# Five edits around the choice of experts: lists by bf16 products, wide products while VectorE works, classes in one comparison, a hinted first jump, the light expert's sum amid a last group

## The chip, the core and the metric

The kernel runs on one core of a Trainium2 chip. A core has a matrix engine (TensorE, PE in the profile, with PEld for its weight loads), VectorE (DVE), ScalarE (ACT), GpSimd (POOL) and SyncE (SP), which here issues the loads of the weights. Each engine has its own program and they meet by semaphores. PEq, DVEq and so on are the sequencers that run an engine's loads of registers and its jumps. The metric is the time of one execution on the device in microseconds; the kernel before took 1330.01 us, the median of three runs (1320.58 to 1333.2).

## The reference

A trunk of two layers on 256 tokens of width 1024, all f32. Each layer is a token mixer (two groups of attention heads) and a channel mixer, each followed by a normalization. The channel mixer of the first layer is a dense SwiGLU; that of the second, which the change touches, sends each token to two of eight experts:

```python
logits = (xf @ router).astype(jnp.float32)
top_v, top_i = lax.top_k(logits, TOP_K)
gates = jax.nn.softmax(top_v, axis=-1)
dense_g = jnp.sum(jax.nn.one_hot(top_i, N_EXPERTS) * gates[..., None], axis=1)
y = jnp.zeros_like(xf)
for e in range(N_EXPERTS):
    y = y + dense_g[:, e:e + 1] * swiglu(xf, wg[e], wu[e], wd[e])
```

An expert's gate and up weights are 1024 x 3584 and its down weights 3584 x 1024.

## The kernel before, in words

The tokens stand in `x_sb`, 128 to a partition block, in two blocks t = 0, 1. After the second normalization of layer 1, `route.logits(t)` transposes a block by eight products with `ident` (L118) and multiplies it with the router (L126); `route.choose(t)` ranks the eight logits on VectorE (L140 to L146) and leaves masks. Between the two stands `route.ones`, 20 bf16 products of 8 columns on PE whose result nobody reads (L133). `route.places` turns the masks into each token's place in the list of its expert, and into counts, by products with triangles (L153 to L157); VectorE then makes from the count of each expert a class from 0 to 5, `kind` (L164 to L167, by comparison with the five BOUNDS 32, 64, 96, 128, 160), and from the logits the gates (L172 to L179). `route.both` makes `pair`, which says whether two experts can be run together.

The experts run in the order of ORDER. For each, a Switch on every engine reads the class from memory into a register (L192) and jumps to the arm for that number of tokens (L1446, L1480): 32 tokens (class 0) to 256 (class 5). At an arm's end `ahead` (L1428) gives each engine's sequencer a hint which arm comes next, so that its code can be fetched ahead of the jump; the first Switch has none. The second and third experts of ORDER, HEAVY and LIGHT, run interleaved (`both`) where their classes allow it.

Inside an arm, for column blocks c = 0, 1 of the hidden width: the gate products (L1090, into "mm" banks of PSUM for few tokens), Silu, the up products (L1090, "acc" banks) and a multiplication, then the hidden rows are transposed (L1123) and the down products made (L1153, or L1023 to L1025 in three passes for classes with 128 tokens at once). The weights come in halves of 1 MB into 18 places in turn. SP loads a half into a place when PE is done with the half that stood there, in one fixed sequence over all experts; `done` is called after each group of halves.

The picked tokens of an expert come into `xg`: for the first one by products of `x_sb` with a one-hot matrix `oh` (L928, `pick`), for each later one by an indirect DMA of rows from `x_rows` into `x_sb` (`gather`, on POOL, L988) and transposes (L996). The gather needs the list of the expert's tokens. `list_tokens` makes all eight lists during the first expert, at its second column block: for each expert VectorE marks the places (L978, f32 128 x 256), and PE multiplies 128 columns of the marks by one column of token numbers (L981, f32), 32 calls. The scheduler that sets the order on each engine spreads these among the gate products of that block, since the marks have two buffers in turn. An expert's result is added to `acc` by `bring`, products with a one-hot matrix (L1010) and four sums on VectorE (L1014), at the head of the next one; the light one's by `bring_light`, handed to the heavy one as `before_end` and called after its last group of down products. After it stand `scatter_few` (L1193 to L1196, for the tokens of HEAVY beyond 128) and the next pick (L996).

In the profiled run the first expert is of class 1 (64 tokens, 447.7 to 541 us), the pair of classes 4 and 0 (549 to 776), and five experts follow, the last of class 0 from 1240.

## Time and profile before

| | |
|---|---|
| median of three runs | 1330.01 us (1320.58 to 1333.2) |
| profiled execution | 1327.82 us, its span 1326.0 us |
| mean granted TensorE clock | 0.970 |
| PE busy | 1267.2 us, 96% of the span |
| DVE, ACT, POOL busy | 459.3 (35%), 360.9 (27%), 45.3 us (3%) |
| DMA | 430.60 MB, mean 325 GB/s |

Rows of the timeline give the start and duration in us, the engine, the line, the operation with output and inputs, the tile of the array and the shape, how many instructions were put together (x), and in brackets how long the engine was idle before and who ended that. An f32 product is recorded as two instructions (the record count is twice that of the calls). The rows of a stretch give the busy time of each engine, the granted clock (1.00 is full speed), the share of time in which the DMA engines were busy, and the bytes they moved. The chain of waits goes back from the last instruction to what released it.

### The profile page before, as it was taken

Reading aid. Unit: us, or ns where it says so; the run is one execution under the profiler, and the core shown is the slowest. Engines: PE = TensorE matmul, PEld = TensorE weight load, DVE = VectorE, ACT = ScalarE, POOL = GpSimd, SP = SyncE. Lnnn points to the kernel's source line nnn. Section 1 sums busy time; section 2 is a strip of 40 time slices with the busy share of each in tenths; the row PEclk is TensorE's granted clock in tenths of the full one; section 3 lists DMA queues with packets and bytes.
Section 4 is the critical chain, followed back from the end, with each engine's and each line's share of the span. In section 5 each row is a group of like instructions: output and inputs, shape, how many; then the busy total and the mean of one; then the engine's idle time right before and its main releaser. Section 6 shows DMA issues by size and latency. Waiting matters only on the chain.

```text
span 1326.0 us, 21614 instructions
## 1 busy us (share of the span) xinstructions
PE 1267.2 (96%) x8971; PEld 777.5 (59%) x8971; DVE 459.3 (35%) x742; ACT 360.9 (27%) x638; POOL 45.3 (3%) x64
## 2 busy tenths in 40 slices
PE   9999999999998799999999999999999999999974
PEld 8978999998987454545665642443542443243331
DVE  4689455567677210336544440001010001000102
ACT  4584444453573100244543410000000000000001
POOL 1010000000001000000000000000000000000000
PEclk9999999999999889999999999999999999999985
DMA  9537455553627899989999979998999999999895
GB/s 331 203 96 258 187 190 182 178 205 136 219 96 302 312 417 406 395 363 410 408 420 418 420 297 377 361 367 330 415 418 415 413 419 415 388 420 412 337 417 241
DMA packets 98026, 430.60 MB, mean 325 GB/s; under 512 B 10403, under 2 KB 16547, under 8 KB 67244
## 3 DMA queue, kind: packets, MB, share of 16 engines
q1 hardware_dynamic: 95804, 422.75, 80.9%
q0 software_dynamic: 2032, 5.63, 1.3%
q8 instruction: 81, 1.33, 0.4%
q14 instruction: 109, 0.89, 0.2%
HBM read 427.73 MB, written 2.11 MB: 324 GB/s over the span
## 4 chain that ended last, share of the span: by engine, by line
PE 82%; DMA 6%; issue 2%; DVE 2%; ACT 1%; POOL 0%; SPq 0%; DVEq 0%; ACTq 0%; POOLq 0%
PE acc L1090 15%; PE acc L1153 15%; PE mm L1090 14%; PE mm L344 4%; PE mm L343 4%; PE mm L345 4%; PE acc L1023 3%; PE acc L345 3%; PE acc L1025 3%; PE acc L344 3%; PE acc L343 3%; PE acc L1024 3%; DMA piece<-in_moe_w_down_dram 3%; PE tr L1123 2%; DMA piece<-in_moe_w_up_dram 1%
## 5 line engine op out<-in xcount | busy, mean ns | idle before, releaser
L1090 PE MATMUL acc<-piece,xg 128*64 128x512 f32 (+5 forms) x1488 | 191.9, 502 | 0.0
L1153 PE MATMUL acc<-piece,hT 128*32 128x256 f32 (+2 forms) x1504 | 175.2, 459 | 8.9 <-DMA piece<-in_moe_w_down_dram 8.9
L307 DVE TENSOR_TENSOR wl<-piece,wh 128x1024 fp32r<-128x1024 f32 (+4 forms) x124 | 135.0, 1098 | 87.9 <-ACT wh L305 85.1
L1090 PE MATMUL mm<-piece,xg 128*64 128x512 f32 (+5 forms) x896 | 143.2, 528 | 15.1 <-issue 5.5
L305 ACT ACTIVATE wh<-piece 128x1024 fp32r<-128x1024 f32 (+4 forms) x124 | 118.1, 958 | 81.6 <-PE acc L344 40.6
L1090 PEld LDWEIGHTS acc<-piece,xg 128*32 128x32 f32 (+1 forms) x1488 | 71.4, 120 | 114.6 <-issue 101.1
L1153 PEld LDWEIGHTS acc<-piece,hT 128*32 128x32 f32 (+1 forms) x1504 | 71.0, 123 | 104.2 <-issue 72.2
L343 PE MATMUL mm<-xTh,wl 128*128 128x256 f32 x448 | 126.7, 283 | 0.0
L344 PE MATMUL mm<-xTh,wh 128*128 128x256 f32 x448 | 126.5, 282 | 0.0
L345 PE MATMUL mm<-xTl,wh 128*128 128x256 f32 x448 | 126.4, 282 | 0.0
L1104 DVE TENSOR_TENSOR hd<-hd,acc 128x512 f32<-128x512 f32 (+1 forms) x24 | 14.5, 630 | 298.7 <-PE acc L1090 297.2
L838 DVE TENSOR_TENSOR wl<-piece,wh 128x1024 fp32r<-128x1024 f32 (+1 forms) x80 | 88.1, 1117 | 76.2 <-PE acc L1025 51.0
L1090 PEld LDWEIGHTS mm<-piece,xg 128*64 128x64 f32 (+1 forms) x896 | 56.9, 131 | 96.2 <-issue 84.7
L1111 ACT ACTIVATE hT<-tr 128x512 f32<-128x512 f32 (+2 forms) x30 | 15.6, 542 | 327.9 <-PE tr L1123 315.2
L837 ACT ACTIVATE wh<-piece 128x1024 fp32r<-128x1024 f32 (+1 forms) x80 | 75.8, 973 | 68.8 <-PE acc L1024 68.6
L343 PEld LDWEIGHTS mm<-xTh,wl 128*128 128x128 f32 x448 | 85.0, 190 | 0.2
L344 PEld LDWEIGHTS mm<-xTh,wh 128*128 128x128 f32 x448 | 84.2, 188 | 0.2
L345 PEld LDWEIGHTS mm<-xTl,wh 128*128 128x128 f32 x448 | 84.2, 188 | 0.0
L1169 DVE COPY hd<-acc 32x256 f32<-32x256 f32 (+2 forms) x12 | 6.6, 554 | 163.4 <-ACT hd L1169 107.5
L343 PE MATMUL acc<-wh,xTl 128*128 128x512 f32 (+2 forms) x128 | 46.7, 365 | 0.0
L345 PE MATMUL acc<-wl,xTh 128*128 128x512 f32 (+2 forms) x128 | 46.3, 363 | 0.0
L344 PE MATMUL acc<-wh,xTh 128*128 128x512 f32 (+2 forms) x128 | 46.2, 361 | 0.0
(474 smaller groups left out, 1648.2 us busy)
## 6 DMA issues: line engine op xcount, KB each, us to landing
piece<-in_moe_w_down_dram SPq DMA_DIRECT2D x95, 1024.0 KB, 15.5
piece<-in_moe_w_gate_dram SPq DMA_DIRECT2D x60, 1024.0 KB, 14.1
piece<-in_moe_w_up_dram SPq DMA_DIRECT2D x58, 1024.0 KB, 16.2
piece<-in_moe_w_up_dram SPq DMA_DIRECT2D x30, 768.0 KB, 10.2
piece<-in_moe_w_gate_dram SPq DMA_DIRECT2D x29, 768.0 KB, 8.5
piece<-in_moe_w_up_dram SPq DMA_DIRECT2D x28, 512.0 KB, 10.1
piece<-in_moe_w_gate_dram SPq DMA_DIRECT2D x26, 512.0 KB, 9.5
piece<-in_ffn_w_gate_dram SPq DMA_DIRECT2D x5, 2048.0 KB, 7.8
```

The costliest lines, as they stand in the source:

```text
L305: hi = act.activation(h, src, AF.Copy)
L307: return hi, dve.tensor_sub(lo, src, h.bitcast(F32))
L343: pe.matmul(ps, lt[1], rt[0], start=start, stop=False)
L344: pe.matmul(ps, lt[0], rt[0], start=False, stop=False)
L345: pe.matmul(ps, lt[0], rt[1], start=False, stop=stop)
L837: act.activation(h, src, AF.Copy)
L838: dve.tensor_sub(lo, src, h.bitcast(F32))
L1023: pe.matmul(ps, lt[1], rt[0], start=start, stop=False)
L1024: pe.matmul(ps, lt[0], rt[0], start=False, stop=False)
L1025: return pe.matmul(ps, lt[0], rt[1], start=False, stop=stop)
L1090: pe.matmul(self.ps[b][q * self.n:(q + 1) * self.n, c0:c0 + (jb - ja) * w], self.tokens(k), block[:, ja - j0:jb - j0, cols], **at)
L1153: latest["down"] = pe.matmul(y[g * self.n:(g + 1) * self.n, c + q:c + q + b], self.hidden(u, j), v[:, j, i * w + q:i * w + q + b], **at)
```

## The change

None of the five edits changes what is computed.

- `route.ones` makes 2 products instead of 20. A new `meanwhile` makes products of 512 columns, f32, whose result nobody reads: three behind the logits of the first block, two behind those of the second, one behind the places.
- `places` hands on the counts. `first` makes the one-hot matrix of the first expert right behind the places; `classes` makes all classes by one comparison of 128 x 40 elements with a tile `bounds` (filled by five memsets on POOL) and one reduction; the gates come after it.
- At the first Switch, the first half of the pick is made, the class of the first expert is loaded on each engine, and a hint is given on each (on PE behind the last product of that half). Then come the second half of the pick, the loads for the other experts, and `pair`.
- The token lists: `mark_tokens` makes all 16 marks in bf16 at the head of the first expert, in a tile "hT" that is free then, and `list_tokens` multiplies them in one go between the gate and the up products of the first column block, by two columns (token number and one). The two gathers for the pair move with it.
- `before_end`, the light expert's sum, is called in the last group of down products after the first part's turn, no more behind the group; and the pick that follows the pair goes to "acc" banks and is copied by ScalarE alone.

```diff
                          pattern=[[1, E], [-1, E]], channel_multiplier=0)
+        self.bounds = tmp.tile([P, len(BOUNDS)], F32, name="bounds")
+        for j, b in enumerate(BOUNDS):
+            gp.memset(self.bounds[:, j:j + 1], b + 0.5)
         self.lg = tmp.tile([P, 2, E], F32, name="lg")
...
         for k in range(KD):
-            pe.matmul(ps[:, :E], xT[:, k], self.rt[:, k], start=k == 0, stop=k == KD - 1)
+            self.latest = pe.matmul(ps[:, :E], xT[:, k], self.rt[:, k], start=k == 0, stop=k == KD - 1)
         return dve.tensor_copy(self.lg[:, t], ps[:, :E])
...
+    def meanwhile(self, tc, ps_pool, ident, x, n):
+
+        ps = ps_pool.tile([P, 512], F32, name="acc")
+        with tc.issue_after(self.latest.ins):
+            for _ in range(n):
+                self.nc.tensor.matmul(ps, ident, x, start=True, stop=True)
+
     def choose(self, t):
...
         pe.matmul(ps[:, 2 * E:3 * E], tri[:, 1], maskb[:, 0], start=True, stop=False)
-        pe.matmul(ps[:, 2 * E:3 * E], tri[:, 1], maskb[:, 1], start=False, stop=True)
+        self.latest = pe.matmul(ps[:, 2 * E:3 * E], tri[:, 1], maskb[:, 1], start=False, stop=True)
         self.pos = pool.tile([P, 2, E], F32, name="pos")
...
-        kf = self.tmp.tile([P, E], F32, name="kf")
-        self.kind = pool.tile([P, E], I32, name="kind")
-        count = ps[:, 2 * E:3 * E]
-        dve.tensor_scalar(kf, count, BOUNDS[0] + 0.5, None, op0=ALU.is_gt)
-        for b in BOUNDS[1:]:
-            dve.scalar_tensor_tensor(kf, count, b + 0.5, kf, op0=ALU.is_gt, op1=ALU.add)
-        dve.tensor_copy(self.kind, kf)
-        self.kf = kf
+        return ps[:, 2 * E:3 * E]
+
+    def first(self, e):
+
+        for t in range(2):
+            self.nc.vector.tensor_scalar(self.oh[:, t], self.iota[:, :P], self.pos[:, t, e:e + 1], self.maskf[:, t, e:e + 1],
+                                         op0=ALU.is_equal, op1=ALU.mult)
+
+    def classes(self, count, heavy, light):
+
+        dve = self.nc.vector
+        over = self.tmp.tile([P, E, len(BOUNDS)], F32, name="over")
+        self.kf = self.tmp.tile([P, E], F32, name="kf")
+        self.kind = self.pool.tile([P, E], I32, name="kind")
+        dve.tensor_tensor(over, count.unsqueeze(2).to_broadcast([P, E, len(BOUNDS)]),
+                          self.bounds.unsqueeze(1).to_broadcast([P, E, len(BOUNDS)]), ALU.is_gt)
+        dve.tensor_reduce(self.kf, over, axis=AX.X, op=ALU.add)
+        dve.tensor_copy(self.kind, self.kf)
+        self.both(heavy, light)
 
+    def weights(self):
+
+        pool, lg, dve, act = self.pool, self.lg, self.nc.vector, self.nc.scalar
         nv = self.tmp.tile([P, 4], F32, name="nv")
...
-    def kinds(self):
-        return [self.nc.values_load(self.kind[0:1, e:e + 1], min_val=0, max_val=len(BOUNDS)) for e in range(self.n)]
+    def load_kind(self, e):
+        return self.nc.values_load(self.kind[0:1, e:e + 1], min_val=0, max_val=len(BOUNDS))
 
...
             if t == 0:
-                route.ones(ps_acc, 20)
-        route.places(ps_tr)
-        route.both(ORDER[HEAVY], ORDER[LIGHT])
+                route.ones(ps_acc, 2)
+            route.meanwhile(tc, ps_acc, ident, x_sb[:, 0, :512], 2 + (t == 0))
+        count = route.places(ps_tr)
+        route.meanwhile(tc, ps_acc, ident, x_sb[:, 0, :512], 1)
+        route.first(ORDER[0])
+        route.classes(count, ORDER[HEAVY], ORDER[LIGHT])
+        route.weights()
         gate.close()
...
             for t in range(2):
-                pe.matmul(tp[:, j * n:(j + 1) * n], src[:, t, (j0 + j) * P:(j0 + j + 1) * P], oh[:, t, :n],
-                          start=t == 0, stop=t == 1)
+                latest["pick"] = pe.matmul(tp[:, j * n:(j + 1) * n], src[:, t, (j0 + j) * P:(j0 + j + 1) * P], oh[:, t, :n],
+                                           start=t == 0, stop=t == 1)
         return tp[:, :kn * n]
...
-    def list_tokens():
+    token = sc.bitcast(BF16)[:, :4].rearrange("p (t c) -> p t c", t=2)
+    pool.memset(token, 1.0)
+    pool.iota(token[:, :, 0], pattern=[[P, 2]], base=0, channel_multiplier=1, allow_small_or_imprecise_dtypes=True)
+
+    def mark_tokens():
 
-        tok = whole("wh", pool_=sp)
-        pool.iota(tok[:, :2], pattern=[[P, 2]], base=-int(NONE), channel_multiplier=1, allow_small_or_imprecise_dtypes=True)
-        ohs, tp = whole("wh", pool_=sp), bank("tr")
+        marks = whole("hT", 2048).bitcast(BF16).rearrange("p (i t n) -> p i t n", t=2, n=S)
         for i, e in enumerate(ORDER[:n_experts]):
-            o = ohs[:, i % 2 * 2 * S:(i % 2 + 1) * 2 * S].rearrange("p (t n) -> p t n", t=2)
             for t in range(2):
-                dve.tensor_scalar(o[:, t], iota, pos[:, t, e:e + 1], route.maskf[:, t, e:e + 1], op0=ALU.is_equal, op1=ALU.mult)
+                dve.tensor_scalar(marks[:, i, t], iota, pos[:, t, e:e + 1], route.maskf[:, t, e:e + 1], op0=ALU.is_equal, op1=ALU.mult)
+        return marks
+
+    def list_tokens(marks):
+
+        tp = bank("tr")[:, :4 * E].rearrange("p (i h c) -> p i h c", h=2, c=2)
+        for i in range(n_experts):
             for h in range(2):
                 for t in range(2):
-                    pe.matmul(tp[:, 2 * i + h:2 * i + h + 1], o[:, t, h * P:(h + 1) * P], tok[:, t:t + 1], start=t == 0, stop=t == 1)
-        dve.tensor_scalar(slot_token, tp[:, :2 * E], NONE, None, op0=ALU.add)
+                    pe.matmul(tp[:, i, h], marks[:, i, t, h * P:(h + 1) * P], token[:, t], start=t == 0, stop=t == 1)
+        to = slot_token.rearrange("p (i h) -> p i h", h=2)
+        dve.tensor_scalar(to, tp[:, :, :, 1], -NONE, NONE, op0=ALU.mult, op1=ALU.add)
+        dve.tensor_add(to, to, tp[:, :, :, 0])
         dve.tensor_copy(slot_row, slot_token)
...
         tp = picked(x_sb, oh, 4 * q) if kind == "tr" else gathered(0, P, 4 * q, 4, kind)
-        (act.copy if q else dve.tensor_copy)(xg[:, q * 512:(q + 1) * 512], tp)
+        (act.copy if q or kind == "acc" else dve.tensor_copy)(xg[:, q * 512:(q + 1) * 512], tp)
 
...
         final = i + 1 == n_experts
+        marks = None if i else mark_tokens()
         parts = [mate] if mate else [Part(xg, *p_) for p_ in CLASSES[cls]]
...
-        def by_turns(units, n, f, between=None):
+        def by_turns(units, n, f, between=None, amid=None):
 
...
                         f(p_, u)
+                    if amid and p_ is turn[0] and u0 + n >= len(units):
+                        amid()
                 turn.reverse()
...
-        def down(c):
+        def down(c, amid=None):
             units = units_of(i, c, 2)
...
                 u, c == 0 and u[3] == 0, c == ds[-1] and u == units[-1],
-                256 if c == ds[-1] and u[3] < narrow and not p_.off else 512), between)
+                256 if c == ds[-1] and u[3] < narrow and not p_.off else 512), between, amid)
 
...
             width = ws[c]
-            if i == 0 and c == cs[-1]:
-                list_tokens()
-                gather(HEAVY, 0)
-                gather(LIGHT, 0, 32, 1)
             if beyond and c == cs[-1]:
...
+                if marks is not None and c == 0 and m:
+                    list_tokens(marks)
+                    gather(HEAVY, 0)
+                    gather(LIGHT, 0, 32, 1)
                 n = abreast(m, c) if paired else 4 if few and c < cs[-1] else len(parts)
...
             gather(i + 2, 0)
-        yield from down(len(ws) - 1)
-        if before_end:
-            before_end()
+        yield from down(len(ws) - 1, before_end)
         for p_ in beyond:
...
         sync.dma_start(x_rows[t * P:(t + 1) * P], x_sb[:, t])
-    kinds = route.kinds()
-    arms = {i: (kinds[e], len(CLASSES)) for i, e in enumerate(ORDER)}
+    kinds, arms = {}, {}
     HEAVY_ARMS = [None, 3, 4]
...
         if i == 0:
-            onehot(oh, e, 0, route.maskf)
-            for q in range(2):
-                pick(q)
+            pick(0)
+            kinds[e] = route.load_kind(e)
+            arms[i] = kinds[e], len(CLASSES)
+            with tc.issue_after(latest["pick"].ins):
+                tc.switch_hint({pe.engine: kinds[e]}, len(CLASSES), "expert0")
+            for x in (act, dve, sync, pool):
+                tc.switch_hint({x.engine: kinds[e]}, len(CLASSES), "expert0")
+            pick(1)
+            for j, e in enumerate(ORDER[1:], 1):
+                kinds[e] = route.load_kind(e)
+                arms[j] = kinds[e], len(CLASSES)
             for t in range(2):
...
             for q in range(2):
-                pick(q, "mm")
+                pick(q, "acc" if i - 1 == LIGHT else "mm")
             bring(sc, ORDER[i - 2 if i - 1 == LIGHT else i - 1])
```

PE at the choice and the first Switch. `tri` is the triangle, `maskb` the masks, `oh` the one-hot matrix; SWITCH_STRIDE and ISA are instructions of the Switch. Before:

```order
L126 MATMUL mm<-rt,xT_4282 128x8 x4
L118 MATMUL tr<-ident,x_sb 128x128 x8
L126 MATMUL mm<-rt,xT_4333 128x8 x8
...
L157 LDWEIGHTS tri
L157 MATMUL tr<-maskb,tri 128x8
L928 MATMUL tr<-oh,x_sb 128x128 x16
L192 TENSOR_LOAD kind
L1439 TENSOR_LOAD pair
L1480 SWITCH_STRIDE
L1480 ISA x2
L1446 BRANCH_PREFETCH_HINT
L1090 MATMUL mm<-piece,xg 32x512 x64
```

After:

```order
L129 MATMUL mm<-rt,xT_4288 128x8 x8
L143 MATMUL acc<-x_sb,ident 128x512 x3
L121 MATMUL tr<-ident,x_sb 128x128 x8
L129 MATMUL mm<-rt,xT_4325 128x8 x8
L143 MATMUL acc<-x_sb,ident 128x512 x2
...
L143 MATMUL acc<-x_sb,ident 128x512
L956 MATMUL tr<-oh,x_sb 128x128 x8
L1475 SWITCH_STRIDE
L216 TENSOR_LOAD kind
L1475 ISA
L1475 BRANCH_PREFETCH_HINT
L956 MATMUL tr<-oh,x_sb 128x128 x8
```

and, after those, up to the first expert's products (of the arm that the scheduler lays first):

```order
L1484 TENSOR_LOAD pair
L1525 SWITCH_STRIDE
L1525 ISA x2
L1491 BRANCH_PREFETCH_HINT
L1127 MATMUL mm<-piece,xg 32x512 x32
```

The wide products stand ahead of the second transposes, of the places and of the pick, each in PE's order; the load of kind stands between the halves of the pick, and the hint with it, where it was behind the whole pick without a hint (the hint at L1446 is given within the jump's own target).

PE in the 64-token arm of the first expert. "mm" are the gate products of a column block, "acc" the up products of the first. Before:

```order
L1090 MATMUL mm<-piece,xg 64x512 x32
L1090 MATMUL acc<-piece,xg 64x512 x32
L981 MATMUL tr<-wh 128x1 x8
L1090 MATMUL mm<-half,xg 64x512 x2
L1090 MATMUL mm<-half,xg 64x256
L981 MATMUL tr<-wh 128x1
L1090 MATMUL mm<-half,xg 64x256 x2
L981 MATMUL tr<-wh 128x1 x4
L1090 MATMUL mm<-half,xg 64x256
L1090 MATMUL mm<-last,xg 64x256
L981 MATMUL tr<-wh 128x1 x4
```

After, the last of the 32 pairs of load and product (hT holds the marks, sc the token numbers) that follow `L1127 MATMUL mm<-piece,xg 64x512 x32`:

```order
L1016 LDWEIGHTS hT
L1016 MATMUL tr<-sc_4416,hT 128x2
L1127 MATMUL acc<-piece,xg 64x512 x32
L1127 MATMUL mm<-half,xg 64x512 x2
L1127 MATMUL mm<-half,xg 64x256 x4
L1127 MATMUL mm<-last,xg 64x256 x4
L1127 MATMUL mm<-last,xg 64x512 x2
L1127 MATMUL mm<-piece,xg 64x256 x2
```

The list's products of one column, spread among the gate products of the second block ("half", "last"), are gone from there, and stand with two columns ahead of the first block's up products.

PE at the end of the pair's arm of class 4. `hT_...` and x_sb are hidden rows of LIGHT, `wh`, `wl` the split weights of HEAVY. Before:

```order
L1025 MATMUL acc<-wl,hT 128x512
L1023 MATMUL acc<-wh,hTl 128x512
L1024 MATMUL acc<-wh,hT 128x512
L1025 MATMUL acc<-wl,hT 128x512
L1010 MATMUL mm<-x_sb,oh 128x512
L1193 MATMUL tr<-h_19219,sc_4420 128x256 x2
L1193 MATMUL mm<-h_19219,sc_4420 128x256 x2
...
L1480 UNCONDITIONAL_BRANCH
L996 MATMUL mm<-ident,x_sb 128x128 x8
L1010 MATMUL tr<-hd,sc_4419 128x512 x2
```

After:

```order
L1190 MATMUL acc<-half,hT_19251 32x256 x8
L1047 MATMUL mm<-x_sb,oh 128x512 x2
L1190 MATMUL acc<-last,hT_19251 32x256 x8
L1060 MATMUL acc<-wh,hTl 128x512
L1061 MATMUL acc<-wh,hT 128x512
L1062 MATMUL acc<-wl,hT 128x512
...
L1062 MATMUL acc<-wl,hT 128x512
L1230 MATMUL tr<-h_19250,sc_4417 128x256 x2
L1230 MATMUL mm<-h_19250,sc_4417 128x256 x2
...
L1525 UNCONDITIONAL_BRANCH
L1033 MATMUL acc<-ident,x_sb 128x128 x8
L1047 MATMUL tr<-hd,sc_4416 128x512 x2
```

Of the four products of the light expert's sum (L1010 before, L1047 after), two go to "tr" and two to "mm" banks. The last of them stood behind all of the group's down products and now stands ahead of HEAVY's part of it. The pick's transposes (L996, L1033) go to "acc".

## The prediction

> **What bounds the kernel now.** I begin with the line of the chain of waits by engine and with the core's line.
>
> ```profile
> core 0: 1326.0 us, clock 0.970
> PE 82%; DMA 6%; issue 2%; DVE 2%; ACT 1%; POOL 0%; SPq 0%; DVEq 0%; ACTq 0%; POOLq 0%
> ```
>
> TensorE holds 82% of the chain. The clock is 0.970 in the mean, so there are stretches at half speed to look for. The kernel also moves 430 MB, so the next question is whether the weight stream or PE sets the pace where the change works, which the busy time per stretch tells.
>
> ```profile
> core 0: us, PE busy (x) PEld busy (x) DVE busy (x) ACT busy (x) POOL busy (x), PEclk, DMA share, GB/s
> 560.00:570.00 10.00, 10.00 (x73) 5.27 (x75) 4.53 (x4) 3.86 (x5) 0.00 (x0) 1.00 0.46 165
> 780.00:790.00 10.00, 9.38 (x44) 3.75 (x48) 4.86 (x8) 0.58 (x1) 1.95 (x2) 1.00 0.25 88
> 910.00:920.00 10.00, 9.98 (x48) 4.10 (x50) 2.80 (x5) 0.15 (x1) 0.00 (x0) 1.00 0.52 178
> 1240.00:1250.00 10.00, 7.95 (x57) 2.61 (x61) 3.84 (x7) 0.58 (x1) 0.00 (x0) 0.83 0.65 226
> 1250.00:1260.00 10.00, 10.00 (x109) 4.49 (x105) 0.69 (x1) 0.60 (x1) 0.00 (x0) 1.00 1.01 403
> ```
>
> The stream stands still in parts of 560 to 570, 780 to 790 and 910 to 920 (shares 0.46, 0.25 and 0.52) while PE is busy throughout: SP issues a half only when PE has given its place back, so there the transfers wait for PE. Only after 1250 is the DMA share full while the last expert runs. From the first dispatch to about 1247, then, PE's own chain is the path, and a microsecond taken out of PE's work comes off the end as long as the stream has standing time left to give. Third, the timeline and the same stretches around the choice of experts.
>
> ```profile
> 423.26 1.04 PE L118 MATMUL tr<-ident,x_sb 128*128 128x128 f32 x8
> 424.14 0.49 PE L133 MATMUL acc<-tri 128*128 128x8 bf16 x14
> 425.65 1.04 PE L126 MATMUL mm<-rt,xT 128*128 128x8 f32 x8
> 429.34 1.94 PE L118 MATMUL tr<-ident,x_sb 128*128 128x128 f32 x8 [2.66 <-DVE x_sb L400]
> 431.21 3.58 PE L126 MATMUL mm<-rt,xT 128*128 128x8 f32 x16
> 436.42 0.17 PE L155 MATMUL tr<-maskb,tri 128*128 128x8 bf16 x1 [1.58 <-DVE maskb L145]
> 437.40 5.41 PE L928 MATMUL tr<-oh,x_sb 128*128 128x128 f32 x32 [0.76 <-DVE nv L177]
> 447.71 15.57 PE L1090 MATMUL mm<-piece,xg 128*64 128x512 f32 x64 [4.90 <-POOL x_sb L988]
> ```
>
> ```profile
> 425.00:430.00 5.00, 2.34 (x23) 2.28 (x23) 3.62 (x10) 0.04 (x2) 0.99 (x1) 0.71 1.01 416
> 430.00:435.00 5.00, 4.84 (x25) 4.45 (x24) 1.68 (x7) 2.57 (x3) 0.00 (x0) 0.50 1.01 416
> 435.00:440.00 5.00, 2.81 (x15) 2.75 (x15) 3.54 (x27) 0.49 (x2) 0.00 (x0) 0.50 1.01 412
> 445.00:450.00 5.00, 2.29 (x6) 0.86 (x8) 1.38 (x4) 0.00 (x0) 1.96 (x3) 0.76 0.11 37
> 450.00:455.00 5.00, 5.00 (x24) 1.73 (x22) 0.00 (x0) 0.00 (x0) 0.00 (x0) 0.90 0.70 216
> ```
>
> The clock is 0.71 between 425 and 430 and 0.50 until 440: eight transposes take 1.94 us where they took 1.04, and sixteen records of router products 3.58 where eight took 1.04. Before the first expert product PE stands 4.90 us, put down to a memset of x_sb. That is a false lead: the product reads piece and xg, not x_sb. What PE does in that time is in the groups of its sequencer.
>
> ```profile
> L1480 PEldq COMPARE_BRANCH  x14: 314/840/3802, 443.5 to 1312.6; - x14
> L192 PEldq TENSOR_LOAD <-kind x8: 298/306/1385, 440.5 to 1111.5; - x8
> ```
>
> (min/median/max in ns, then the first and last start.) The first jump starts at 443.5 and, being the longest at 3.80 us, ends at 447.3, just ahead of the product at 447.71. It alone had no hint; the median of all is 0.84.
>
> **The change part by part.** *A1, the hinted dispatch.* Before, 447.71 - 437.40 = 10.31 us from the pick's first product to the expert's. After, PE's sequencer has the first half of the pick, the load of kind, the hint, the second half, the load of pair and the jump. Before, it reached the kind load 3.1 us after the pick began (440.5 - 437.4), so a half of the pick is 1.6. I take 1.6 + 1.4 (the longest load) + 1.6 + 1.1 for the pair's load (between 0.3 and 1.4) + 0.8 for a hinted jump = 6.5. The fetch, 3.80 - 0.84 = 3.0, has 1.6 + 1.1 = 2.7 of cover, so 0.3 is left: 6.8, which is 3.5 less. Bounds: 0 (the hint has no effect) to 4.0. The pick itself, 5.41, still ends ahead of that. DVE, ACT, SP and POOL load the one kind and have their own hints; none is waited for before PE's jump.
>
> *A2, the clock until the pick.* Eighteen narrow products go and 3 + 2 + 1 wide ones come, in PE's order ahead of the transposes, the places and the pick. One is two records of f32, 128x512; the rows at the end of the pair, below, show four such records in 1.72 us, so a call is 0.86 at full clock, 1.72 at half. They have the idle time of PE to hide in: 2.58 in 2.66, 1.72 in 1.58, 0.86 in 0.76; over by 0.24 in all at full clock, by 5.4 at half (2.5 + 1.9 + 1.0). If the clock holds, the transposes are 0.9 shorter and the router's sixteen records 3.58 - 2 x 1.04 = 1.5 shorter: 2.2 net. If not, up to 5.4 longer. Whether the second group starts at full clock is not certain, so I take 1.2 less, nearer the gain, since the longest gap is nearly filled.
>
> The falls of the clock come with stretches of few or narrow products (425 to 430: 23 records, then 0.50). The Trainium skill (TensorE: Matmul & The Clock Gate, Part 1: The HAM clock gate (the "warmup" mystery)) has the window at about 3.4 us and free-running, and half speed after an idle one; this trace agrees as to the 0.71 and 0.50 above, and by that rule the gain of A2 would change from run to run with where the window falls.
>
> *A3, the first gate products.* With no idle of 4.9 us before them they begin at full speed. Their cost at full speed is that of the next sixty-four, in the chain:
>
> ```profile
> 447.71 15.57 PE mm L1090 x64
> 463.28 13.73 PE acc L1090 x64
> ```
>
> 15.57 - 13.73 = 1.8 less; bounds 0 to 1.8.
>
> *B, the token lists.* The gate of the second column block now has the list's products among its own, and the same stage of a later expert of the same class has none.
>
> ```profile
> 476.90:504.00 27.10, 27.10 (x138) 16.41 (x137) 5.85 (x17) 0.00 (x0) 2.11 (x2) 0.75 0.98 401
> 937.70:948.10 10.40, 10.40 (x74) 6.01 (x70) 0.69 (x1) 0.00 (x0) 0.00 (x0) 1.00 1.03 419
> L981 PE MATMUL tr<-wh x64: 250/250/373, 476.9 to 495.8; 128*128 128x1 f32 x64
> 448.48 1.38 DVE L978 TENSOR_SCALAR wh<-iota,pos,maskf 128x256 f32<-128x256 bf16 x4 [6.73 <-issue]
> ```
>
> 138 records against 74, the difference being the 64 of the list, and 27.10 us at clock 0.75 against 10.40 at 1.00: 16.7 us is what the list costs, its own 64 x 0.25 = 16.0 and the clock that the narrow products lose for the work around them. What comes is 32 bf16 products with a load each. Nearest are the fourteen bf16 products above, 0.49 / 14 = 0.035 each (loaded alike): 32 x 0.035 = 1.1; by the old list's 0.25 it would be 8.0. I take 1.2: 15.5 less, bounds 8.7 to 15.6. Their 16 marks cost DVE 16 x 1.38 / 4 = 5.5 us. If DVE starts no sooner than at 448.48 they are done at 454.0, and PE comes to them after the gate products, at 437.4 + 6.8 + 13.7 = 457.9: hidden, by 3.9 at the least. Behind the burst on PE stands all of "up". The two gathers move ahead with the list; POOL issues them, on a queue of its own, into a stream with a share of 0.70 between 450 and 455, and they are read only by the pair at about 550: nothing. The five memsets of the bounds are on POOL, which is 3% busy, ahead of the choice: nothing.
>
> *C, the end of the pair.* Last waits there:
>
> ```profile
> 776.75 0.75 DVE L1014 SCALAR_TENSOR_TENSOR acc<-mm,gate,acc 128x512 f32<-128x512 f32 x1 [1.05 <-PE mm L1010]
> 778.94 1.29 DVE acc L1196 x2
> 780.62 1.06 PE mm L996 x8
> 783.41 1.72 PE acc L1010 x4
> ```
>
> The last product of the light bring (0.86) and its sum (0.75) leave the tail, and the next pick, in "acc" banks now, need not wait for the sums of L1196 in "mm". Of 780.62 - 778.94 = 1.7 plus 0.86, 2.6 at most, I take 1.5; bounds 0 to 2.6. What is moved forward puts two sums of 0.75 between DVE's splits for the last group, by which PE could wait as long: hence the 0.
>
> Sum: 3.5 + 1.2 + 1.8 + 15.5 + 1.5 = 23.5. The profiled execution took 1327.8 (span 1326.0), which gives 1304.3. It is 2.2 under the median of 1330.0, so the median comes to 1306.5.
>
> Has the stream 23.5 to give before 790? The shares above say it stands 4.5 + 1.5 (445 to 455) + 5.4 + 7.5 = 18.9. The missing 4.6 comes out of the lead of landed halves that the standing at 780 to 790 proves (18 halves, all full), some two halves of 2.4 us, and is won back where the stream stands later.
>
> **The rivals.** *R1: the wide products run at half speed,* because the window at 425 already counted as idle. Then A2 costs 5.4 instead of saving 1.2, with A1, A3, B and C kept: 23.5 - 6.6 = 16.9, median 1313. For it: 0.71 in 425 to 430. Against: the gap that lowers the clock is the one that is filled. *R2: the hint does nothing.* 23.5 - 3.5, and 1.8 more because the clock falls again: 18.2, 1312. Against: later jumps, hinted at the end of the arm before, have a median of 0.84; there the hint also stands some instructions ahead of the jump. The Trainium skill (Runtime: NRT & Kernel Launch, Instruction fetch mechanics) says that a taken branch out of the two pages held forces a fetch; by that rule the hint's page could be displaced by the second half of the pick, and this is the rival it stands for; the 3.80 here agrees with the fetch, no run here shows the displacement. *R3: the stream is the bound after all* and gives only its standing time: 18.9, 1311. Against: PE stays busy at 780 to 790 with a full ring. *R4: the list's price only moves,* each load at 0.25 and the clock falling behind it: 8.7 from B less 1.8, sum 14.9, 1315. *R5, slower: PE stands at the burst until DVE has made all 16 marks.* "Up" is behind it, and SP's refills behind that. If the marks came as late as the last of the old list (495.8), PE would stand 495.8 - 457.9 = 37.9: 14.4 slower, 1344. It costs from marks at 457.9 on, and eats the whole gain from 481 on. Against: DVE has nothing else to do from 450 to 455 (0.00 above).
>
> **How the numbers follow.** Forecast 0.58, R1 0.14, R2 0.11, R3 0.08, R4 0.06, R5 0.03. The likeliest gives 1306.5. Its low end is all upper bounds, 4.0 + 2.2 + 1.8 + 15.6 + 2.6 = 26.2, 1303.8, less two other falls of the clock of a half window of 3.4 us each that may not come, say 4: 1300. The high end takes in R1 to R3 and R4's 1315, with 3 more for a median that is itself between 1320.58 and 1333.2 in three runs: 1318. About 1% (13.3 us, 1316.7) is what a measurement tells from no change: the forecast, R1 to R3 and half of R4 are 0.94, of which I move 0.09 to the cases in which two of R1 to R4 meet and less than 13 is left: faster 0.85, same 0.12, slower 0.03.
>
> **What would show it.** Right: the first expert product 6 to 7.5 us after the pick's first; PEclk 1.00 from 425 on; the list's 32 products within 1 to 3 us, and the gate of the second block near 10.4; the next pick after the pair without a wait for DVE. Wrong: a jump of over 2 us at the first Switch (R2); wide products of over 1 us (R1); PE waiting for a weight DMA before 790 (R3); a list of over 5 us (R4); idle PE before it put down to DVE (R5).

## The result, and the profile after

The changed kernel takes 1317.03 us (median of 17 runs, 1312.98 to 1320.08) against 1328.33 (17 runs, 1320.58 to 1333.89): the ratio is 0.9915, 95% interval 0.99 to 0.993. That is 11.3 us less, where 23.5 were forecast. Its profiled execution has a span of 1317.1 us, 8.9 less than that of before.

The changed kernel's chain of waits by engine, and its core's line:

```profile
PE 82%; DMA 5%; issue 3%; DVE 2%; ACT 1%; POOL 0%; DVEq 0%; ACTq 0%; SPq 0%; POOLq 0%
```

```profile
core 0: 1317.1 us, clock 0.976
```

PE still holds 82% of the chain; the share of "issue" went from 2% to 3%, and the clock is 0.976 in the mean where it was 0.970.

The timeline of PE around the choice and the first expert (L121 are the transposes, L129 the router's products, L143 the wide ones, L956 the pick, L1127 gate and up, L1016 the list, L1160 the turning of the hidden rows):

```profile
423.45 1.03 PE L121 MATMUL tr<-ident,x_sb 128*128 128x128 f32 x8
426.58 2.82 PE L143 MATMUL acc<-x_sb,ident 128*128 128x512 f32 x6
429.38 1.29 PE L121 MATMUL tr<-ident,x_sb 128*128 128x128 f32 x8
430.79 1.95 PE L129 MATMUL mm<-rt,xT 128*128 128x8 f32 x16
435.49 3.81 PE L956 MATMUL tr<-oh,x_sb 128*128 128x128 f32 x32
444.31 16.34 PE L1127 MATMUL mm<-piece,xg 128*64 128x512 f32 x64 [5.01 <-DVE hT L1007]
460.59 0.95 PE L1016 MATMUL tr<-sc,hT 128*128 128x2 bf16 x32
461.47 13.95 PE L1127 MATMUL acc<-piece,xg 128*64 128x512 f32 x64
485.69 1.22 PE L1160 MATMUL tr<-ident,hd 128*128 128x128 f32 x8
```

The wide products end in time for what follows, the transposes and the router's products run at full speed, the list takes 0.95 us, and from the second gate stage on nothing of the list is left. But PE stands 5.01 us ahead of the first gate product, as long as before (4.90), and those products take 16.34. The stretches of that time show the clock:

```profile
core 0: us, PE busy (x) PEld busy (x) DVE busy (x) ACT busy (x) POOL busy (x), PEclk, DMA share, GB/s
430.00:435.00 5.00, 4.84 (x31) 3.38 (x31) 3.49 (x21) 2.98 (x5) 0.24 (x2) 1.00 1.01 416
440.00:445.00 5.00, 0.69 (x2) 0.32 (x4) 1.11 (x5) 0.00 (x0) 0.00 (x0) 0.73 1.01 385
445.00:450.00 5.00, 5.00 (x16) 1.62 (x14) 4.32 (x13) 0.00 (x0) 1.95 (x2) 0.58 0.53 145
475.30:485.70 10.40, 10.40 (x75) 5.00 (x71) 0.79 (x2) 0.00 (x0) 0.00 (x0) 1.00 1.01 420
```

It is 1.00 through the choice, and falls in the idle time that is still there. What PE waits for is named in the row as the marks on VectorE (L1007). That is as false as the memset was before, since the product reads `piece` and `xg` and not the marks: the jump of PE's own sequencer lasts 6.10 us and ends just ahead of the product. Two more jumps are long where they weren't, the one into the pair and the one out of it. The sequencer's jumps one by one, first of the changed kernel (at 437.8, 527.0 and 765.3), then of the kernel before at the same three places; the columns are min/median/max in ns, which are one number here, and the start:

```profile
L1525 PEldq COMPARE_BRANCH  x1: 6103/6103/6103, 437.8 to 437.8; - x1
L1525 PEldq COMPARE_BRANCH  x1: 6057/6057/6057, 527.0 to 527.0; - x1
L1525 PEldq COMPARE_BRANCH  x1: 5618/5618/5618, 765.3 to 765.3; - x1
```

```profile
L1480 PEldq COMPARE_BRANCH  x1: 3802/3802/3802, 443.5 to 443.5; - x1
L1480 PEldq COMPARE_BRANCH  x1: 408/408/408, 543.7 to 543.7; - x1
L1480 PEldq COMPARE_BRANCH  x1: 2185/2185/2185, 778.2 to 778.2; - x1
```

With the starts of PE's products at the borders of the stages, read from both timelines, the spans of these two executions divide like this (us):

| stage | before | after | difference | forecast |
|---|---|---|---|---|
| transposes of the first block to the pick (A2) | 14.1 | 12.0 | -2.1 | -1.2 |
| pick to the first gate product (A1) | 10.3 | 8.8 | -1.5 | -3.5 |
| gate products, with the list's 0.9 after (A3) | 15.4 | 17.2 | +1.8 | -1.8 + 1.2 |
| up, and gate of the second block (B) | 40.9 | 24.2 | -16.7 | -16.7 |
| from there to the pair's first product | 44.7 | 47.6 | +2.9 | 0 |
| the pair to its last down product | 226.9 | 231.4 | +4.4 | 0 |
| to the next pick (C) | 5.0 | 6.7 | +1.7 | -1.5 |
| to that expert's first product | 4.4 | 7.1 | +2.7 | 0 |
| to the last jump | 451.3 | 451.6 | +0.3 | 0 |
| the last expert and the end | 89.6 | 87.1 | -2.5 | 0 |

Up to the turning of the hidden rows (485.69 against 504.00) 18.3 us were gained, of 22.0 expected there. Nearly two thirds of it were given back in the next four rows: 2.9 + 4.4 + 1.7 + 2.7 = 11.7.

### The profile page after: what moved, and what is told of

Its sections match the earlier page's. It is cut to its first block, busy times and chain, and to the rows that moved or that the text cites. A ratio compares the mean times of both kernels' runs of the same rounds, so it can differ in the third digit from the quotient of the medians.

```text
span 1317.1 us, 21562 instructions
## 1 busy us (share of the span) xinstructions
PE 1255.7 (95%) x8933; PEld 766.4 (58%) x8933; DVE 458.9 (35%) x739; ACT 361.7 (27%) x639; POOL 45.8 (3%) x70
## 4 chain that ended last, share of the span: by engine, by line
PE 82%; DMA 5%; issue 3%; DVE 2%; ACT 1%; POOL 0%; DVEq 0%; ACTq 0%; SPq 0%; POOLq 0%
PE acc L1127 16%; PE acc L1190 15%; PE mm L1127 14%; PE mm L368 4%; PE mm L367 4%; PE mm L369 4%; PE acc L1060 3%; PE acc L369 3%; PE acc L1062 3%; PE acc L367 3%; PE acc L368 3%; PE acc L1061 3%; DMA piece<-in_moe_w_down_dram 3%; DMA piece<-in_moe_w_up_dram 2%; PE tr L1160 2%
## 5 line engine op out<-in xcount | busy, mean ns | idle before, releaser
L1127 PE MATMUL acc<-piece,xg 128*64 128x512 f32 (+5 forms) x1488 | 192.0, 502 | 0.0
L1127 PE MATMUL mm<-piece,xg 128*64 128x512 f32 (+5 forms) x896 | 138.2, 514 | 16.3 <-issue 5.7
L1127 PEld LDWEIGHTS acc<-piece,xg 128*32 128x32 f32 (+1 forms) x1488 | 71.0, 120 | 114.4 <-issue 98.4
L1141 DVE TENSOR_TENSOR hd<-hd,acc 128x512 f32<-128x512 f32 (+1 forms) x24 | 14.5, 630 | 286.8 <-PE acc L1127 285.2
L1127 PEld LDWEIGHTS mm<-piece,xg 128*64 128x64 f32 (+1 forms) x896 | 56.4, 128 | 96.6 <-issue 83.4
## 6 DMA issues: line engine op xcount, KB each, us to landing
piece<-in_moe_w_up_dram SPq DMA_DIRECT2D x28, 512.0 KB, 10.2
```

The costliest lines, as they stand in the source:

```text
L1127: pe.matmul(self.ps[b][q * self.n:(q + 1) * self.n, c0:c0 + (jb - ja) * w], self.tokens(k), block[:, ja - j0:jb - j0, cols], **at)
```

## The experiments

The theory that I took up from the table, called F below: a jump waits for a packet of code; while the stream of weights is full, that packet comes some 3.5 us after it is asked for; and whether it has been asked for in time depends on where the code lies and how much work stands ahead of the jump. Idle time at a jump then also lowers the clock. Rivals: the weight stream is the bound and gives only a part (S), and falls of the clock that go with the parts, or with the place of the clock's window alone (K).

### The lists alone

On the kernel before, with the new `mark_tokens` and `list_tokens` of the change in place of the old list:

```diff
-            if i == 0 and c == cs[-1]:
-                list_tokens()
-                gather(HEAVY, 0)
-                gather(LIGHT, 0, 32, 1)
...
+                if marks is not None and c == 0 and m:
+                    list_tokens(marks)
+                    gather(HEAVY, 0)
+                    gather(LIGHT, 0, 32, 1)
```

> The kernel before with the token lists alone as the change has them (16 marks at the head of the first expert, 32 bf16 products in one go, gathers earlier). In the changed kernel's profile this part saved 16.6 us up to the end of the first expert (27.1 us became 10.4 in the second gate stage), but of 18.4 us gained there 8.9 reached the end. Theory F (late code): what is lost is lost at jumps, because PE's next 16-KB packet of code waits behind the full weight stream; here the first jump stays as before (3.8 us, no hint), and the time falls by 15 to 16 if the jumps into the pair and out of it stay as short as before (0.4 and 2.2), and by 3 to 6 less for each one that is 5 to 6 us long. Rival S (the weight stream is the bound and gives only a part): the same 8 to 11 us less whatever the jumps do. Rival K (the loss comes with the other parts: light sum amid the group, clock): 15.5 less, jumps aside.

1317.73 us, ratio 0.992 (0.989 to 0.995): about the whole of the change's gain (0.9915), with one of its parts. Up and second gate stage took 24.21 us as in the changed kernel. The first jump was 4.41 us, the one out of the pair 2.34, but the one into the pair was long although nothing of the dispatch, the bring or the classes had been edited:

```profile
L1490 PEldq COMPARE_BRANCH  x1: 6092/6092/6092, 530.4 to 530.4; - x1
```

A fall of the clock that lasted 10.2 us (755.4 to 765.7) lay near the end of the pair as in the changed kernel (749.5 to 759.8). The other four parts together add nothing that can be measured. S says the same time, so this run alone doesn't separate it from F.

### The code shifted, nothing more executed

```diff
+        if i == 0 and cls == 5:
+            spare = bank("tr")
+            for _ in range(32):
+                pe.matmul(spare[:, :P], ident, ident, start=True, stop=True)
```

> The changed kernel with 32 products put into an arm of the first expert that is not taken in this run (256 tokens): nothing more is executed, but all of PE's code behind it lies 128 instructions (8 KB) further on, half a packet. Theory F with the place of the code in its 16-KB packets as the cause: the jump at 526.98 (6.06 us) falls below 1.5 and the stop of 1.6 us ahead of it goes, so the pair's first product comes about 3 us sooner (the sums on VectorE hold it otherwise); the jump out of the pair (5.62 us) changes too, to about 2 if the packet is asked for sooner. In all 3 to 6.5 us less than the changed kernel. Rival (the full stream alone makes them long, or the hint is dropped for another reason): both jumps stay at 5.5 to 6.1, no difference.

1312.93 us, ratio 0.9871 (0.9832 to 0.991). The jump into the pair:

```profile
L1529 PEldq COMPARE_BRANCH  x1: 402/402/402, 528.1 to 528.1; - x1
```

6.06 us became 0.40 with no instruction more on the way: the place of the code decides this one. The packets of PE's code (queue q8, 16 KB each) show what differs. In the changed kernel one comes at 522.95, 3.6 us behind the hint at 519.32 and well ahead of the jump at 526.98; but the jump ends only after the next one, which comes at 530.56, 3.6 us behind the jump's start. With the shift the one behind the hint, at 525.65, is enough: the jump at 528.1 does not wait for the next, at 531.84. From the turning to the pair's first product it takes 44.8 instead of 47.6, the rest being hidden behind the sums on VectorE (L1051), as expected. The jump out of the pair did not become shorter (5.90), against the expectation. The ratio's interval overlaps the changed kernel's (0.99 to 0.993), so the whole time is not shown to be lower. S falls for this stage: the bytes are the same.

### No hint at the first Switch

```diff
-            with tc.issue_after(latest["pick"].ins):
-                tc.switch_hint({pe.engine: kinds[e]}, len(CLASSES), "expert0")
-            for x in (act, dve, sync, pool):
-                tc.switch_hint({x.engine: kinds[e]}, len(CLASSES), "expert0")
```

> The changed kernel without its hints at the first Switch, on all five engines. Prediction's step A1: the hint covers most of the fetch, so without it the first product comes 2.7 us later or more. Theory F: the hint stands only 0.98 us ahead of PE's jump and the fetch takes 6.1 us while the stream is full; without it at most 1 us later, or none at all (then the hint did nothing here); the packet of PE's code comes about 3.6 us after the jump in both.

1320.47 us, ratio 0.994 (0.9911 to 0.997), which overlaps the changed kernel's. From the pick's first product to the expert's it took 9.89 us against 8.82, and the jump 6.56 against 6.10:

```profile
L1521 PEldq COMPARE_BRANCH  x1: 6557/6557/6557, 440.5 to 440.5; - x1
```

Two more profiles of kernels that have the hint (9.53 with the shift, 9.50 in the repetition below) made their pick when this one did (437.6 and 437.4 for 437.5), where the changed kernel's came 2.0 us sooner. Like with like, then, the hint is worth 0.4 us, and 1.1 at the most, as F has it, not the 2.7 and more of step A1. In the changed kernel the packet begins 3.6 us behind the jump's start, just as the unhinted second packet at the pair does; here, without a hint, it is 3.9. So that the hint was followed at all, with 0.98 us ahead of the jump, is not shown.

### The light expert's sum behind the group again

```diff
-        (act.copy if q or kind == "acc" else dve.tensor_copy)(xg[:, q * 512:(q + 1) * 512], tp)
+        (act.copy if q else dve.tensor_copy)(xg[:, q * 512:(q + 1) * 512], tp)
...
-        yield from down(len(ws) - 1, before_end)
+        yield from down(len(ws) - 1)
+        if before_end:
+            before_end()
...
-                pick(q, "acc" if i - 1 == LIGHT else "mm")
+                pick(q, "mm")
```

> The changed kernel with the light expert's sum behind the whole last group again, and the next pick in the mm banks with one copy on VectorE, as before. Prediction's step C: 1.5 us slower than the changed kernel. Theory F: the tail is 2 us longer, but the packet that the jump out of the pair waits for is asked for at the same time or sooner, so the jump is shorter by as much: no difference, or up to 3 faster, with the jump near 2.2. Rival K: the long fall of the clock at 749.5 to 759.8 goes with the sum's move and this is 3 us faster with the jump unchanged.

1313.33 us, ratio 0.9905 (0.9868 to 0.9943), an interval that holds the changed kernel's 0.9915: by the time the two cannot be told apart. PE at the end of the pair, with the sum amid the group (the changed kernel) and behind it:

```profile
765.35 0.38 PE L1230 MATMUL mm<-h,sc 32*128 32x256 f32 x2
771.33 1.94 PE L1033 MATMUL acc<-ident,x_sb 128*128 128x128 f32 x8 [5.59 <-issue]
```

```profile
761.88 0.79 PE L1230 MATMUL mm<-h,sc 32*128 32x256 f32 x3
764.80 1.94 PE L1033 MATMUL mm<-ident,x_sb 128*128 128x128 f32 x8 [2.14 <-DVE acc L1233]
```

The scatter's products end 1.1 us behind the last down product with the sum amid and 3.0 behind it with the sum at the end, but then PE stands 5.59 us for its code and not 2.14 for VectorE: the gap from the last down product to the next pick is 6.67 against 5.16. In the six other profiles with the sum amid it was 6.85, 6.63, 6.99, 6.56, 7.05 and 4.96; in the three others with the sum behind, besides the list alone (5.12), 5.24, 4.79 and 5.03. The pair's stage had no fall of 10 us here and took 225.6 us for 231.4, which is more than the 3.7 us between the two medians; the repetition below bears on whose that is.

### The stream paused during the first jump

```diff
-    for q in range(len(halves)):
+    for q in range(len(halves) - 4):
         fetch(q)
...
+            if i == 0:
+                for q in range(len(halves) - 4, len(halves)):
+                    fetch(q)
```

> The changed kernel with the last 4 of the first 18 halves of weights asked for only in the first expert's arm, so that the stream is let up while the engines fetch the code of that arm. Theory F: the packet of PE's code comes about 1.5 us after it is asked for instead of 3.6 to 4.6, the first jump lasts 3 to 4 us instead of 6.1, and the first product comes 6.5 to 7.5 us after the pick's first instead of 8.8; 2 to 3 us less than the changed kernel if no weights are missed later. Rival (five engines that fetch at once hold one another up, or a hinted fetch is as long anyhow): the jump stays near 6.

The stretches ahead of the first jump and across it (the last two columns are the DMA share and GB/s), and the jump itself:

```profile
440.00:442.00 2.00, 2.00 (x20) 2.00 (x19) 0.94 (x9) 0.00 (x0) 0.00 (x0) 1.00 0.00 0
442.00:446.00 4.00, 1.56 (x15) 1.40 (x15) 0.95 (x4) 0.58 (x1) 1.83 (x2) 1.00 0.05 16
```

```profile
L1528 PEldq COMPARE_BRANCH  x1: 3377/3377/3377, 442.1 to 442.1; - x1
```

With the stream at rest (shares 0.00 and 0.05) the jump took 3.38 us, the first product came 6.19 us after the pick's first, and the gate stage with the list took 14.77: 5.0 us less than the changed kernel up to the first up product. So it is the full stream that makes the fetch long; five engines fetch at once here too, and that alone does not make it 6 us. The time was 1320.42 all the same, ratio 0.9934 (0.9911 to 0.9956): the way from the turning to the pair's first product took 53.26 us instead of 47.62, and 3.0 us of the difference are waits for weights (where the rest comes from is not shown). PE's waits between 484 and 533 (us in all, times, longest) name them, where the changed kernel has no such row:

```profile
PE acc L1190 <- DMA piece<-in_moe_w_down_dram: 3.0, 4, 1.2
```

Here S is right: without the list's 16 us the first expert has little of the stream to spare.

### The idle time filled

```diff
             pick(1)
+            route.latest = latest["pick"]
+            route.meanwhile(tc, ps_acc, ident, x_sb[:, 0, :512], 5)
```

> The changed kernel with five more wide products (4.3 us at full clock) behind the second half of the first pick, in PE's idle time of 5 us before the first expert product. Step A3 of the prediction (the clock holds over the first gate products where PE has no idle time): the gate stage goes from 16.3 to 13.9 us, 2.4 less, and the fall of the clock at 442 to 449 is gone. If the clock falls for another reason, the stage stays at 16 and nothing is gained.

1314.15 us, ratio 0.9887 (0.9834 to 0.994). The gate stage, of the changed kernel and with the filling:

```profile
444.30:460.60 16.30, 16.29 (x65) 5.48 (x65) 5.01 (x15) 0.72 (x1) 1.95 (x2) 0.85 0.86 309
```

```profile
447.60:462.40 14.80, 14.76 (x96) 6.27 (x96) 4.61 (x16) 1.57 (x2) 1.89 (x2) 1.00 0.84 303
```

(The second stretch includes the list.) The clock stays at 1.00, and gate with list takes 14.77 instead of 17.16: 2.4 less, as expected. It is the idle time at the jump that cost step A3. The twenty instructions more also shifted the code, and the jump into the pair was 0.40 us.

### The narrow products again

```diff
-                route.ones(ps_acc, 2)
-            route.meanwhile(tc, ps_acc, ident, x_sb[:, 0, :512], 2 + (t == 0))
+                route.ones(ps_acc, 20)
...
-        route.meanwhile(tc, ps_acc, ident, x_sb[:, 0, :512], 1)
```

> The changed kernel with the 20 narrow products as before and no wide ones. Step A2 (1.2 to 2.2 us of it): the clock falls at 427 for four windows as before, the second transposes and router products take 5.5 instead of 3.2 us, and the first pick begins about 2 us later; the time is 2 longer. If the clock is a matter of the window's place alone, no difference.

1321.43 us, ratio 0.9956 (0.9933 to 0.9979), 4.4 more than the changed kernel. The stretch from the first transposes to the pick, of this kernel, of the changed one, of the one with the shift and of the one with the filling (whose products there are the changed kernel's):

```profile
423.10:437.20 14.10, 9.14 (x74) 8.54 (x73) 9.16 (x33) 4.17 (x7) 1.23 (x3) 0.71 1.01 419
```

```profile
423.40:435.50 12.10, 11.69 (x69) 7.65 (x67) 9.35 (x34) 4.06 (x7) 1.23 (x3) 1.00 1.02 419
```

```profile
424.10:437.60 13.50, 12.90 (x68) 8.27 (x67) 9.23 (x34) 4.17 (x7) 1.23 (x3) 0.87 1.01 416
```

```profile
424.30:439.40 15.10, 14.51 (x68) 9.11 (x67) 9.78 (x39) 4.17 (x7) 1.24 (x3) 0.77 1.01 419
```

14.1 us with the narrow products in all three kernels that have them. With the wide ones it is 12.0 where the clock holds, 13.6 with one fall and 15.2 with two: the fall makes the wide products themselves long, and they stand ahead of what PE needs. Up to the pick the wide products gain 2.1 or lose 1.1 with the same instructions. Up to the first gate product they never lost: from the first transposes to there it took 20.1 to 23.4 us in the ten profiles with wide products and 24.4, 24.9 and 25.1 in the three with narrow ones (24.9 here, 10.79 of it behind the pick, although this kernel has the hint).

### The shift and the sum behind the group together

Both edits as above, on the changed kernel (the next pick's banks and copies go back too, not shown again):

```diff
+        if i == 0 and cls == 5:
+            spare = bank("tr")
+            for _ in range(32):
+                pe.matmul(spare[:, :P], ident, ident, start=True, stop=True)
...
-        yield from down(len(ws) - 1, before_end)
+        yield from down(len(ws) - 1)
+        if before_end:
+            before_end()
```

> The shift of the code by 128 instructions and the light expert's sum behind the group together, on the changed kernel. Theory F with the place of the code: the jump into the pair 0.4 us and the one out of it 2.3, so the gap from the last down product to the next pick near 5.0 (6.7 to 6.9 with the sum amid); each alone measured about 4 less than the changed kernel, of which some 1.7 each is theirs by the jumps and the rest the clock's; together 4 to 6 less than the changed kernel. Rival K (the differences of both are the clock's place alone): no more than either.

1313.61 us, ratio 0.9904 (0.9871 to 0.9937), no better than either alone, though both effects are in the profile: the jumps are 0.40 and 2.46 us and the gap to the next pick 5.24. Its profiled execution was the shortest so far (span 1309.9). As to the time, the rival has it right: the medians of these three lie within 0.7 us, which is nothing that four to seven runs of each could tell.

### Shift, sum and filling

That kernel, with the filling too:

```diff
             pick(1)
+            route.latest = latest["pick"]
+            route.meanwhile(tc, ps_acc, ident, x_sb[:, 0, :512], 5)
```

> The shift of the code, the sum behind the group and the five wide products behind the first pick together. Theory F with the clock as a consequence of the idle time at the jumps: against the kernel with shift and sum alone (gate stage 16.8 us, 8.85 from the pick to the first product) the gate stage is 14.8 and the rest stays: 2 less than that, some 5 to 6 less than the changed kernel, with the pair's stage at 225 to 226. Rival K (the clock's place decides, whatever is filled): the differences drown in falls at other places, and the time is that of the shifted kernels, 1313.

1309.71 us, ratio 0.9845 (0.9818 to 0.9872). The timeline of the jump:

```profile
435.01 3.81 PE L956 MATMUL tr<-oh,x_sb 128*128 128x128 f32 x32
438.66 4.46 PE L143 MATMUL acc<-x_sb,ident 128*128 128x512 f32 x10
443.04 13.96 PE L1127 MATMUL mm<-piece,xg 128*64 128x512 f32 x64
```

No idle time, and the gate at 13.96 as at full speed. The ratio's interval lies under the changed kernel's (0.99 to 0.993). It overlaps that of the changed kernel's repetition below (0.9855 to 0.992), but all six runs here (1306.94 to 1312.68) are under all four there (1313.98 to 1319.31), taken side by side. So the three edits together do gain over the change. The pair's stage, against the expectation of 225 to 226, was 231.7, with a fall from 745.4 to 755.6 although the sum stood behind the group.

The hint can be read once more here. The jump (4.00 us) stands 2.1 us behind it, and the code's packet begins 1.5 us behind the jump. In the filling alone and with the narrow products, where 3.3 and 3.7 us lie between hint and jump, the packet begins 1.1 and 2.6 us behind the jump (the latter as the stream was already stopping). In the five profiles with 1 us between them and the stream running, it was 3.5 to 4.4. That speaks for a hint being followed when it stands further ahead.

### The changed kernel once more

> The changed kernel itself once more. What the code's place does comes again to within 0.3 us: the jumps into the pair and out of it at 6.0 and 5.6. What the clock's windows do need not: if the fall of 10 us near the end of the pair is a matter of where the window lies, the pair's stage (231.4 us from its first product to its last down product) may be 226 here and the first pick may lie 2 us later after a fall at 427; if it belongs to the change, it is there again.

1315.46 us, ratio 0.9888 (0.9855 to 0.992). The jumps into the pair and out of it:

```profile
L1525 PEldq COMPARE_BRANCH  x1: 5872/5872/5872, 528.9 to 528.9; - x1
L1525 PEldq COMPARE_BRANCH  x1: 4078/4078/4078, 768.0 to 768.0; - x1
```

The first came again (5.87); the second was 4.08 instead of 5.62, outside the 0.3 us that I had allowed, and the gap to the next pick 4.96, no longer than before the change. The pair's stage, of before, of the changed kernel and of this repetition:

```profile
548.70:775.70 227.00, 225.27 (x1653) 132.66 (x1654) 116.95 (x123) 97.55 (x121) 3.83 (x4) 0.98 0.99 405
```

```profile
533.30:764.70 231.40, 229.70 (x1656) 134.55 (x1657) 116.41 (x121) 97.62 (x121) 4.02 (x4) 0.97 1.02 416
```

```profile
535.10:767.50 232.40, 230.70 (x1656) 135.30 (x1656) 116.26 (x121) 97.72 (x120) 3.98 (x4) 0.96 1.02 416
```

The long stage came again with its fall (753.6 to 763.9). But over the kernels it goes with no part: the list alone, no hint, stream paused, filling and narrow products had 231.0 to 232.6, the shift 226.3, the sum behind the group 225.6 and with the shift 225.4, and shift, sum and filling 231.7. The pick lay 1.7 us later, after a fall at 432.8 that the first profile did not have.

The starts and ends of the falls tell more. In each profile they all lie on one grid with a step of 3.41 us. PE stands 0.91 us just ahead of the first product of the light expert's sum (L1047, near 748 in the changed kernel), and whether the clock falls there goes with how long before that product a step of the grid ends (the twelve profiles so far and that of the next section):

| light expert's sum | step's end ahead of its first product, and the fall that follows |
|---|---|
| amid the group | 0.9, 1.2, 1.7, 1.7, 1.9 and 1.9 us: 10.2 us each; 2.4 us: none |
| behind the group | 0.9 and 0.9 us: 10.2 us each; 1.5 and 1.5 us: 3.4 us each; 2.2 and 2.5 us: none |

So whether the fall comes, and at 0.9 us its length too, goes with where PE's arrival lies on the grid and not with an edit. At 1.5 to 1.9 us it was 3.4 with the sum behind and 10.2 with the sum amid; no two profiles of the two kinds have the same place there, so whether the sum's move lengthens it stays open.

### A brief pause

The kernel with shift, sum and filling, with three wide products behind the pick for five, and two halves asked for late. In the arm not taken stand 34 products for 32 (that line is not shown), so that the code behind it lies the same:

```diff
-    for q in range(len(halves)):
+    for q in range(len(halves) - 2):
         fetch(q)
...
-            route.meanwhile(tc, ps_acc, ident, x_sb[:, 0, :512], 5)
+            route.meanwhile(tc, ps_acc, ident, x_sb[:, 0, :512], 3)
...
+            if i == 0:
+                for q in range(len(halves) - 2, len(halves)):
+                    fetch(q)
```

> The kernel with shift, sum behind the group and filled fetch, with three wide products in place of five and the last 2 of the first 18 halves asked for in the first expert's arm (with 4 the first jump was 3.4 us, but PE stood 3.0 us for weights at the end of the first expert). Theory F: the code's packet comes sooner, the first product 6.2 to 7 us after the pick's first instead of 8.0, the gate stage stays at 14.8, and with half the pause no wait for weights comes at the end of that expert: 1 to 2 less than the kernel without the pause. Rival S (the first expert now lives at the limit of the stream): any pause is paid back in full before the pair, no difference or slower.

```profile
L1536 PEldq COMPARE_BRANCH  x1: 1685/1685/1685, 441.4 to 441.4; - x1
```

1307.74 us, ratio 0.9863 (0.9839 to 0.9887). The jump took 1.69 us, the first product came 6.24 us after the pick's first, the gate stage with the list took 14.77, and PE waited for no weights in the first expert: as F expected. Its time is the lowest measured, but its ratio's interval overlaps that of the kernel without the pause (taken beside other runs of the kernel before), so that the pause is worth anything in the end is not shown.

## Why the prediction was right, and where it was wrong

The time lies in the range, 1.0 us under its upper end, and by a way that was not the forecast's: 11.3 us were gained, of 23.5. That the range held it is luck. Its upper end was put together from the cases of R1 to R4, and most of what used up the gain stood in none of them. By the prediction's own threshold of about 1% (1316.7 us) this is still "the same", to which it gave 0.12; that the kernel did become faster follows from the ratio's interval, 0.99 to 0.993. In the two profiled executions some 14.5 us of the forecast are missing: 2.0 in A1, 2.4 in A3, 3.2 in C and 10.0 in stages to which the sum gave nothing, less 0.9 that A2 gave beyond its term and about 2 at the end.

**What bounds the kernel.** PE's chain was the path, as read: the list's 16.7 us were whole at 485.69. That the stream could give them without PE waiting also held, but with less to spare than the prediction's two halves of lead suggested: asking for four halves late brought a wait of 3.0 us. The stream did not take the gain back (R3): PE waited for no weights between 430 and 800, and between 740 and 800 it was busy for 0.81 of the time, less than before (0.87), while PE stood for its code.

**A1, the hint, failed** at two terms. The cover was put at 2.7 us, with half a pick's time on PE taken for the sequencer's; PE's sequencer had the second half of the pick issued and pair loaded within 0.98 us of the hint (the loads of kind and pair took 0.49 and 0.32 us, not 1.4 and 1.1), 1.5 us before the pick's last product ended. And the fetch, put at 3.0 of a jump of 3.80 that came as the stream was just about to stand still, was that of a jump of 6.10 when it came 5.7 us earlier, into a full stream. In the DMA's account of the changed kernel, from the hint to 441.4 (436.9 to 441.4, the first two rows) and from there to 442.6 (the others), the one packet of queue q8, 16 KB, comes in the second stretch, 4.6 us after the hint and 3.6 after the jump; the jump ends 1.4 us behind it:

```profile
q1 hardware_dynamic: 475, 1.79, 99.5%
q14 instruction: 1, 0.01, 0.4%
```

```profile
q1 hardware_dynamic: 103, 0.39, 94.1%
q8 instruction: 1, 0.02, 5.8%
```

The prediction's reading that an earlier jump is an earlier start was wrong for that reason: of 5.7 us that the jump came sooner, 3.4 were kept. Of the rivals R2 came nearest: its sign, a jump of over 2 us, is there, and the hint was worth 0.4 to 1.1 us or nothing. The Trainium skill (Runtime: NRT & Kernel Launch, Instruction fetch mechanics) has a taken branch outside the pages held wait for a fetch by DMA; the runs agree, with a first jump of 3.4 us with a resting stream and 6.1 to 6.9 with a full one. That the second half of the pick displaces the hinted page is not shown.

**A2, the wide products:** the term of 1.2 was 2.1 in this profile, and 0.5 or -1.1 in others: inside the bounds, and its spread was foreseen, since by the Trainium skill (TensorE: Matmul & The Clock Gate, Part 1: The HAM clock gate (the "warmup" mystery)) the window is free-running; three lengths of one piece of code, 12.0, 13.6 and 15.2, and the grid of the falls agree with that. R1 is thus not a case beside the forecast but a draw at each run.

**A3 failed** with A1: the idle time of 5.0 us stayed, and the clock fell in it; 0.9 us lost instead of 1.8 gained. Filling the idle time gave it back.

**B was right** in place and size: 15.5 less forecast, 16.7 - 0.95 = 15.8 measured, the same 24.21 in nine of the eleven other profiles and 24.22 in two. R4 and R5 are out: the burst took 0.95 us and PE did not stand for the marks.

**C failed** in sign in the profiled run (+1.7 for -1.5): PE's tail became 2.0 us shorter (3.0 to 1.1), but what was late next was the packet of code for the way out of the pair (it begins 3.7 us behind the last down product, with the sum behind the group 2.2), which the longer tail had covered. In one of the seven profiles with the sum amid the gap was not longer.

**What the sum did not have:** the jump into the pair (+2.9 at the pair's first product), the half speed behind the jump out of the pair (+2.7), and the pair's stage (+4.4). The first was shown to be the code's place. For the second, the clock is at 0.50 from 770.0 to 776.9, behind the idle time at the jump; but the length of that jump does not make it. Of the five kernels whose jump there took 2.0 to 2.5 us, as it did before, four needed 7.0 to 7.4 us for this row and one 6.1, and two with jumps of 5.5 and 5.9 needed 5.9 and 6.0. So its cause is not shown. The third goes with the long fall, and that with the place of the clock's grid, as the table in the repetition shows. A fall of the clock at 1242.9 that the kernel before had and the changed one has not lies in the -2.5 of the last row; the rest of it is not explained.

## What to carry to other kernels

A jump is paid in code that must come through the same DMA engines as the data: before a jump is counted, look at how full the stream is at that moment, and put independent work there rather than rely on a hint a microsecond ahead. A pause of the stream shortened the jump too, but no gain in the whole time was shown for it, and the longer pause brought waits for weights. An edit anywhere moves all the code behind it, so compare the jumps one by one in both profiles before a gain or a loss is put down to the edit; a few instructions in an arm that is not run tell the two apart. A gain on the path must be followed to the end through each later wait that was covered by what went.
